# Row maxima of 80 attention branches scaled by ScalarE instead of VectorE in a two-layer decoder trunk

## The chip, the cores and the metric

One core of one Trainium2 chip runs the whole program. The metric is device microseconds (us) from start to end of one execution, and the median of several executions is compared. The engines are called by the profile's names: PE (TensorE; PEld is its weight load), DVE (VectorE), ACT (ScalarE), POOL (GpSimd) and SP (SyncE, which issues the DMAs).

## The reference, cut to what matters

A two-layer decoder trunk runs over 1024 tokens of width 1024 in float32. Layer 0 mixes sparse attention (compressed, selected and windowed branches) with sink attention. Layer 1 mixes three dilated patterns. Each layer ends in a SwiGLU FFN. Each attention branch is a softmax over masked scores, and the change concerns the row maximum in it:

```python
s = jnp.einsum('bhgqd,bhkd->bhgqk', qr_b, kw, preferred_element_type=jnp.float32) * SCALE
s = jnp.where(wmask, s, -jnp.inf)
o_win = jnp.einsum('bhgqk,bhkd->bhgqd', jax.nn.softmax(s, axis=-1), vw.astype(jnp.float32))
...
    m = jnp.max(s, axis=-1)
    if sink is not None:
        m = jnp.maximum(m, sink)
    p = jnp.exp(s - m[..., None])
```

## The kernel before

The tokens are worked in two halves of 512. Dense jobs (projections, output projections, FFN) form one stream of matmuls. The attention branches are woven into that stream in four phases: layer 0 first half, layer 0 second half, layer 1 first half, layer 1 second half. Each phase has its own list of branches:

- kind B, 8 in each half of layer 0: sink attention;
- kinds A and W, 8 each in each half of layer 0: selected blocks and the 512 window;
- kind cmp, 8 in each half of layer 0: compressed blocks (in the first half they come last);
- kind C, 16 in the first half of layer 1;
- kinds G and N, 16 each in the second half of layer 1: strided and near keys.

That makes 112 branches with a row of maxima each: 16 of kind B, 16 of cmp, and 80 of A, W, C, G and N.

For a branch, `s_issue` (line 1639) makes PE write a unit of scores to one of two PSUM banks called pS. `maxima` (line 1659) then reduces them on DVE. For all kinds but cmp, the fused operation of line 1684 adds the mask and takes the maximum over a row, starting from `FLOOR`, in one instruction (a CUSTOM_DVE instruction and a read of its accumulator in the trace). The result is a column of the small tile `m8` (SM in the trace). When the last unit is reduced, line 1700 makes a tensor_scalar on DVE: the maximum with `FLOOR` (or with the sink), times 1/STEP, written as 128x4 float16 into the tile `br["m"]` (MR in the trace). For A and W in the second half a row's scores come in two parts, so a tensor_max (line 1697) runs first.

PE then transposes MR by a matmul with the identity into a pS bank (line 1706), ACT copies that to a tile NM (line 1709), and SP writes it as a row behind the branch's queries (line 1712). Then the branch's scores are made again, transposed and with that row, and ACT takes their exponentials.

The order of every engine's instructions is fixed when the program is built, by a planner in the kernel file. Each step is a generator that yields the letter of the engine it wants next ("v" DVE, "a" ACT, "p" PE, "vg" DVE or POOL, "s" SP). `run` (line 380) always advances the step that can start first, on clocks that `account` (line 298) keeps from the cost tables of lines 257 to 259. So a step that asks for another engine shifts the planned clocks of both engines, and with them the order of everything planned later. On the chip each engine works through its list in order, and semaphores make it wait where the plan was too early.

Of the kernel before, what the change touches and what calls it, by code (L numbers as in the profile page):

```python
# [15 lines left out]
AF = mybir.ActivationFunctionType  # L16
ALU = mybir.AluOpType
# [19 lines left out]
FLOOR = -1.25e9  # L37
STEP = 32768.0
# [223 lines left out]
class Kernel:  # L262
# [1396 lines left out]
    def maxima(self, br, h, u, fin, s):  # L1659

        nc = self.nc
        if "m" not in br:
            br["m"], br["mb"] = self.MR.take(), self.SM.take()
        m8 = br["mb"].t
        np_ = br.get("np", 1)
        if br["kind"] == "cmp":
            yield "v", self.TM.when
            sm = self.TM.take()
            nc.vector.tensor_tensor(sm.t, s.t[:, 0:256].rearrange("p (b c) -> p b c", c=64),
                                    self.mCmp[:, h * HB:(h + 1) * HB], op=ALU.add)  # L1670
            s.drop()
            yield "v"
            nc.vector.tensor_reduce(out=m8[:, 0:HB], in_=sm.t, axis=AX.X, op=ALU.max)
            sm.drop()
        else:
            mc = m8[:, 0:HB * np_].rearrange("p (b c) -> p b c", c=np_)
            tab = br["maskS"] if hasattr(br["maskS"], "shape") else br["maskS"]()
            x = 0
            for il, a, w, c, left in u:
                acc = mc[:, il, c:c + 1]  # L1680
                yield "v"
                if tab.shape[1] >= left:
                    o = tab.shape[1] - left
                    nc.vector.tensor_tensor_reduce(out=self.junk[:, 0:w], in0=s.t[:, x:x + w], in1=tab[:, o:o + w],
                                                   scale=1.0, scalar=FLOOR, op0=ALU.add, op1=ALU.max, accum_out=acc)
                else:
                    nc.vector.tensor_reduce(out=acc, in_=s.t[:, x:x + w], axis=AX.X, op=ALU.max)
                x += w
            s.drop()
            br["parts"] -= 1  # L1690
            if br["parts"]:
                return
        yield "v"
        top = m8[:, 0:HB]
        if np_ > 1:

            nc.vector.tensor_max(mc[:, :, 0], mc[:, :, 0], mc[:, :, 1])
            top = mc[:, :, 0]
            yield "v"
        nc.vector.tensor_scalar(br["m"].t, top, br["sink"][1] if "sink" in br else FLOOR, 1.0 / STEP, op0=ALU.max,  # L1700
                                op1=ALU.mult)
        br["mb"].drop()
        row = self.low(br)[64 + br["row"]:65 + br["row"]]
        yield "p", self.pS.when
        ps = self.pS.take()
        nc.tensor.matmul(ps.t[0:HB, 0:P], br["m"].t, self.ident16, start=True, stop=True)
        yield "a", self.NM.when
        nm = self.NM.take()
        nc.scalar.copy(nm.t, ps.t[0:HB, 0:P])
        ps.drop()  # L1710
        yield "s"
        self.dma(row.rearrange("r (b p) -> r b p", b=HB), nm.t)
        nm.drop()
        br["ready"] = self.scope + self.o.rowlat
# [1105 lines left out]
```

## Time and profile before

| | us |
|---|---|
| median of 3 runs | 2656.15 |
| range of the runs | 2652.08 to 2656.83 |
| the profiled execution, its own time | 2659.92 |
| span of the profiled execution, first to last instruction | 2658.1 |
| mean granted TensorE clock, of full speed | 0.975 |

All work of the kernel carries one line of the code (L245) in the profile, since a helper issues it, so the groups below are told apart by engine, operation and tile: MR is the tile of scaled maxima, SM small tiles, pS, pT, pO and pD PSUM banks, S working tiles in SBUF, and PH the two halves of the probabilities. A "wait" is idle time of an engine, put down to the work that ended last before it went on.

### The profile page before, as it was taken

The page shows a single profiled execution, that of the slowest core. Times are in us where ns is not written, and L with a number is a line of the kernel's source. Part 1 is how long each engine was busy: PE and PEld are TensorE (multiplying, and loading weights), DVE is VectorE, ACT ScalarE, POOL GpSimd, SP SyncE. Part 2 cuts the span into 40 slices and gives each one's busy share as a digit, 9 for nine tenths or more (in the row PEclk, how much of TensorE's full clock was granted, in tenths as well). Part 3 has the DMA queues.
Part 4 walks back from the last instruction along what each step waited for, and adds up shares of the span by engine and source line. Part 5 has one row for each costly group of instructions (what it writes and reads, how often), then busy time and mean ns, then how long its engine had stood idle before and what let it go on. Part 6 is the DMA issues. An engine that isn't in the chain of part 4 may idle for free.

```text
span 2658.1 us, 42701 instructions
## 1 busy us (share of the span) xinstructions
PE 2514.3 (95%) x15510; PEld 1586.3 (60%) x15510; DVE 1959.7 (74%) x4445; ACT 1437.0 (54%) x2398; POOL 720.1 (27%) x511
## 2 busy tenths in 40 slices
PE   7887889899999999999999999998999999999998
PEld 7665667655555577765444477766555557754445
DVE  6798988877887788686666667888787885555554
ACT  6555656666666566544444456555566665433332
POOL 3344555301011344441000144334011114500002
PEclk8898999999999999999999999998999999999999
DMA  6465355222233234643334346685255443533320
GB/s 172 137 170 133 115 162 154 70 84 79 84 89 89 82 115 155 207 130 102 111 97 118 105 139 184 165 222 162 81 149 144 132 141 104 174 119 100 103 80 32
DMA packets 456214, 331.63 MB, mean 125 GB/s; under 512 B 54310, under 2 KB 431344, under 8 KB 456004
## 3 DMA queue, kind: packets, MB, share of 16 engines
q1 hardware_dynamic: 456004, 328.91, 42.8%
q8 instruction: 122, 2.00, 0.3%
q14 instruction: 88, 0.72, 0.1%
HBM read 273.41 MB, written 51.09 MB: 122 GB/s over the span
## 4 chain that ended last, share of the span: by engine, by line
PE 42%; DVE 9%; issue 3%; ACT 2%; DMA 2%; POOL 1%; SPq 1%; DVEq 0%; POOLq 0%; ACTq 0%
PE pD L245 38%; DVE S L245 6%; PE pS L245 2%; ACT S L245 1%; PE pT L245 1%; PE pO L245 1%; DVE SM L245 1%; POOL S L245 1%; DVE pT L245 1%; DVE junk L245 1%; SPq L245 1%; DMA S<-in_w_out_o 1%; DMA S<-xd 0%; DVE PH L245 0%; DMA S<-in_w_out_e 0%
## 5 line engine op out<-in xcount | busy, mean ns | idle before, releaser
L245 PE MATMUL pD<-S,S 128*128 128x512 f16 (+3 forms) x9648 | 2196.5, 379 | 28.6 <-DVE S L245 23.7
L245 PEld LDWEIGHTS <-S 128*128 128x128 f16 (+2 forms) x6960 | 644.6, 100 | 712.4 <-issue 87.1
L245 PEld LDWEIGHTS pD<-S,S 128*128 128x128 f32 x4272 | 732.5, 193 | 160.9 <-DVE S L245 17.4
L245 POOL TENSOR_TENSOR S<-S,S 128x512 f32<-128x512 f32 (+3 forms) x261 | 480.2, 1853 | 819.8 <-ACT S L245 682.4
L245 DVE SCALAR_TENSOR_TENSOR S<-S,wsc,S 128x1024 f16<-128x1024 f32 x224 | 295.2, 1318 | 59.3 <-ACT S L245 57.2
L245 ACT ACTIVATE S<-S 128x1024 f16<-128x1024 f32 (+4 forms) x294 | 238.1, 811 | 133.4 <-DVE S L245 131.8
L245 ACT CAST S<-S 128x512 fp32r<-128x512 f32 (+2 forms) x251 | 241.1, 1016 | 102.1 <-DVE S L245 59.0
L245 ACT ACTIVATE S<-S,wsc 128x1024 f16<-128x1024 f32 x224 | 253.5, 1141 | 50.0 <-DVE wsc L245 45.5
L245 DVE SCALAR_TENSOR_TENSOR S<-pD,SM,S 128x512 f32<-128x512 f32 x208 | 156.1, 751 | 130.1 <-PE pD L245 119.7
L245 DVE TENSOR_TENSOR S<-S,S 128x512 fp32r<-128x512 f32 (+3 forms) x149 | 191.8, 1299 | 62.0 <-ACT S L245 58.0
L245 POOL TENSOR_TENSOR PH<-S,PH 128x512 f16<-128x512 f32 (+3 forms) x76 | 94.8, 1249 | 455.5 <-ACT PH L245 323.2
L245 DVE TENSOR_TENSOR S<-pD,S 128x512 f32<-128x512 f32 (+1 forms) x238 | 157.3, 665 | 69.5 <-PE pD L245 62.3
L245 DVE TENSOR_TENSOR PH<-S,PH 128x512 f16<-128x512 f32 (+3 forms) x228 | 168.0, 741 | 43.1 <-ACT PH L245 42.0
L245 ACT ACTIVATE S<-pD,SM 128x512 f32<-128x512 f32 (+2 forms) x136 | 80.4, 604 | 198.0 <-PE pD L245 168.5
L245 ACT CAST PH<-S 128x512 f16<-128x512 f32 (+3 forms) x304 | 175.9, 586 | 9.4 <-PE pO L245 2.6
L245 PE MATMUL pT<-S,S 128*128 128x128 f16 (+11 forms) x1072 | 167.3, 279 | 11.6 <-ACT S L245 8.3
L245 ACT ACTIVATE S<-pT,jointC 128x512 f32<-128x512 f32 (+1 forms) x112 | 73.2, 655 | 165.4 <-DVE pT L245 163.8
L245 PEld LDWEIGHTS <-PH 128*128 128x128 f16 (+1 forms) x3384 | 128.3, 100 | 54.1 <-issue 16.4
L245 ACT ACTIVATE S<-pT,jointA 128x512 f32<-128x512 f32 (+1 forms) x144 | 92.1, 648 | 116.0 <-DVE pT L245 87.6
L245 PE MATMUL pO<-S,PH 128*128 128x65 f16 (+1 forms) x3192 | 133.7, 197 | 12.3 <-DVE PH L245 5.6
L245 POOL TENSOR_TENSOR S<-OS,SM 128x256 f32<-128x256 f32 x57 | 50.4, 884 | 341.2 <-DVE SM L245 291.4
L245 PE MATMUL pS<-S,S 128*128 128x256 f16 (+4 forms) x460 | 98.8, 302 | 20.4 <-DVE SM L245 14.9
(216 smaller groups left out, 1997.7 us busy)
## 6 DMA issues: line engine op xcount, KB each, us to landing
S<-in_w_gate_up SPq DMA_DIRECT2D x176, 512.0 KB
S<-in_w_down SPq DMA_DIRECT2D x88, 512.0 KB
S<-in_w_qkv_o SPq DMA_DIRECT2D x48, 512.0 KB
S<-in_w_in_e SPq DMA_DIRECT2D x22, 512.0 KB
xd<-S SPq DMA_DIRECT2D x32, 256.0 KB
S<-in_w_out_e SPq DMA_DIRECT2D x16, 512.0 KB
S<-xd SPq DMA_DIRECT2D x32, 256.0 KB
S<-in_w_out_o SPq DMA_DIRECT2D x16, 512.0 KB
```

Of the source, the lines that this page charges most:

```text
L245: return fn(*a, **kw)
```

## The change

The scaling of line 1700 is given to ACT for the branches that have neither a sink nor kind cmp (A, W, C, G and N). It becomes an activation Copy with scale 1/STEP. The maximum with `FLOOR` is left out there, since the fused operation starts from it. The yields before it ask for ACT instead of DVE. The tensor_max of two parts stays on DVE.

```diff
-        yield "v"
+        yield "v" if np_ > 1 or "sink" in br or br["kind"] == "cmp" else "a"
         top = m8[:, 0:HB]
         if np_ > 1:
 
             nc.vector.tensor_max(mc[:, :, 0], mc[:, :, 0], mc[:, :, 1])
             top = mc[:, :, 0]
-            yield "v"
-        nc.vector.tensor_scalar(br["m"].t, top, br["sink"][1] if "sink" in br else FLOOR, 1.0 / STEP, op0=ALU.max,
-                                op1=ALU.mult)
+            yield "v" if "sink" in br else "a"
+        if "sink" in br or br["kind"] == "cmp":
+            nc.vector.tensor_scalar(br["m"].t, top, br["sink"][1] if "sink" in br else FLOOR, 1.0 / STEP, op0=ALU.max,
+                                    op1=ALU.mult)
+        else:
+            nc.scalar.activation(br["m"].t, top, AF.Copy, scale=1.0 / STEP)
         br["mb"].drop()
```

## Rows read from the trace of the kernel before

**Rows 1.** The page's first two parts: busy time of each engine with its share of the span and its instructions, and the granted TensorE clock in 40 slices of the span.

```profile
PE 2514.3 (95%) x15510; PEld 1586.3 (60%) x15510; DVE 1959.7 (74%) x4445; ACT 1437.0 (54%) x2398; POOL 720.1 (27%) x511
...
PEclk8898999999999999999999999998999999999999
```

**Rows 2.** Busy time of the engines by stage: stretch, its length, then busy us and instructions of PE, PEld, DVE, ACT and POOL, the granted clock, the DMA share and GB/s. 181 to 346 is kinds A and W of the first half of layer 0, 475 to 1000 the second half (A, W, cmp), 1000 to 1143 projections, 1143 to 1745 kind C and 1745 to 2184 kinds G and N.

```profile
181.00:346.00 165.00, 136.57 (x1065) 98.42 (x1063) 146.57 (x347) 102.18 (x187) 87.15 (x61) 0.93 0.48 126
...
475.00:1000.00 525.00, 512.33 (x3626) 296.27 (x3625) 417.68 (x1078) 342.54 (x572) 115.79 (x89) 1.00 0.30 88
1000.00:1143.00 143.00, 134.94 (x729) 110.56 (x728) 107.76 (x185) 80.99 (x110) 67.74 (x40) 0.99 0.56 178
1143.00:1745.00 602.00, 579.49 (x3292) 360.84 (x3291) 429.10 (x783) 283.34 (x420) 141.79 (x91) 0.99 0.46 131
1745.00:2184.00 439.00, 422.96 (x2829) 249.92 (x2826) 358.56 (x1001) 271.27 (x477) 91.90 (x77) 0.97 0.51 142
```

**Rows 3.** The same columns in stretches of 10 us inside the first of these stages.

```profile
250.00:260.00 10.00, 4.74 (x50) 3.42 (x48) 9.92 (x19) 6.63 (x11) 8.37 (x6) 0.96 0.78 185
260.00:270.00 10.00, 7.75 (x44) 5.33 (x45) 7.59 (x13) 6.39 (x14) 2.16 (x2) 0.69 0.62 179
...
310.00:320.00 10.00, 5.82 (x31) 3.57 (x29) 9.82 (x16) 6.07 (x14) 10.00 (x6) 1.00 0.20 52
320.00:330.00 10.00, 9.15 (x69) 6.64 (x70) 8.89 (x28) 4.75 (x10) 1.54 (x4) 0.83 0.42 112
```

**Rows 4.** Instructions that write or read the tile MR, by stage: PE, PEld, DVE and ACT busy, then clock, DMA share and GB/s. Up to 1143 the DVE instructions here are writes of MR alone.

```profile
181.00:346.00 165.00, 3.35 (x15) 1.20 (x15) 8.75 (x15) 0.83 (x2) 0.93 0.48 126
346.00:394.00 48.00, 1.96 (x9) 0.72 (x9) 3.49 (x9) 0.00 (x0) 0.98 0.54 167
...
475.00:1000.00 525.00, 5.22 (x24) 1.93 (x24) 8.64 (x24) 0.88 (x3) 1.00 0.30 88
```

**Rows 5.** Instructions that write or read MR in the whole span: count, then min/median/max of the duration in ns, first and last start, and form.

```profile
L245 DVE TENSOR_SCALAR MR<-SM x96: 134/167/1568, 181.1 to 2182.6; 128x4 f16<-128x4 f32 x96
...
L245 ACT ACTIVATE SM<-MR,sinks,jointB x16: 389/391/426, 129.2 to 503.0; 128x4 f32<-128x4 f16 x16
L245 ACT CAST OG<-MR x16: 198/201/207, 1745.6 to 2210.3; 128x4 f32<-128x4 f16 x16
```

**Rows 6.** Groups of instructions by form: count, busy us, mean ns of one, idle before.

```profile
L245 DVE TENSOR_SCALAR MR<-SM 128x4 f16<-128x4 f32 x96 | 33.5, 348 | 0.7
```

**Rows 7.** Waits of PE in 181 to 346: total us, times, longest.

```profile
PE pS L245 <- DVE MR L245: 8.9, 3, 3.8
PE pT L245 <- ACT S L245: 5.0, 5, 2.7
PE pS L245 <- DVE SM L245: 3.9, 6, 0.8
PE pO L245 <- DVE PH L245: 3.7, 5, 1.0
```

**Rows 8.** Waits in the whole span: PE on the tile MR, on DVE's reductions (which free the pS banks) and on ACT, and ACT on DVE.

```profile
PE pS L245 <- DVE SM L245: 36.5, 30, 6.3
PE pS L245 <- DVE MR L245: 12.4, 9, 3.8
PE pT L245 <- ACT S L245: 9.3, 10, 2.7
PE pS L245 <- ACT S L245: 8.1, 3, 5.6
...
ACT S L245 <- DVE pT L245: 276.7, 155, 7.9
```

**Rows 9.** Timeline around the first long wait of PE on MR: start, duration, engine, operation, count, and in brackets the idle time before with its releaser.

```profile
255.67 6.50 POOL L245 TENSOR_TENSOR S<-S,S 128x512 fp32r<-128x512 f32 x3
...
256.39 0.39 ACT L245 ACTIVATE S<-pD 127x256 f32<-127x256 f32 x1
...
256.94 0.07 DVE L245 DVE_READ_ACCUMULATOR2_ANT SM<- 128x1 f32 x1
256.94 4.10 DVE L245 TENSOR_TENSOR S<-S,S 128x512 fp32r<-128x512 f32 x2
...
260.96 1.23 DVE L245 TENSOR_SCALAR MR<-SM 128x4 f16<-128x4 f32 x1
262.11 0.62 DVE L245 TENSOR_TENSOR pT<-pT,tDE 128x128 f32<-128x128 f32 x2
...
262.25 0.26 PE L245 MATMUL pS<-ident,MR 128*4 128x128 f16 x1 [3.72 <-DVE MR L245]
262.43 0.69 ACT L245 ACTIVATE S<-pT,jointA 128x512 f32<-128x512 f32 x1 [5.64 <-DVE pT L245]
```

**Rows 10.** The same around the second and the third long wait.

```profile
290.18 0.08 DVE L245 DVE_READ_ACCUMULATOR2_ANT SM<- 128x1 f32 x1
290.30 0.82 DVE L245 TENSOR_SCALAR MR<-SM 128x4 f16<-128x4 f32 x1
...
291.18 0.22 PE L245 MATMUL pS<-ident,MR 128*4 128x128 f16 x1 [1.33 <-DVE MR L245]
...
318.94 1.22 DVE L245 TENSOR_SCALAR MR<-SM 128x4 f16<-128x4 f32 x1
318.98 0.37 ACT L245 COPY OS<-pO 128x260 f32<-128x260 f32 x1
...
320.21 0.22 PE L245 MATMUL pS<-ident,MR 128*4 128x128 f16 x1 [3.80 <-DVE MR L245]
```

## The prediction

> **What bounds the kernel now.** I read the page's busy times first. PE is busy 95% of the span, DVE 74%, ACT 54% [rows 1]. So a microsecond is gained only where PE idles or where its clock is below full. Next I read the stages. From 475 to 1000 PE is busy 512.33 of 525 us, and from 1143 to 2184 it lacks 39 us of 1041. In 181 to 346, however, it lacks 28.4 of 165 us, DVE is busy 146.57 (89%), POOL 87.15, and the granted clock is 0.93 [rows 2]. That is the first phase, where kinds A and W run, and it is the one stage in which the step to be moved plainly holds PE. There PE waits 8.9 us in three pieces for DVE's write of MR, the largest entry of its list [rows 7], of 12.4 us in nine pieces over the whole span [rows 8]. Last I read the timeline around those three waits [rows 9, 10], to see why DVE was late.
>
> The step is cheap when nothing disturbs it, 0.134 us at the least and 0.167 us at the median, but it has taken up to 1.568 us [rows 5]. Over 96 writes the mean is 0.348 us, in sum 33.5 us [rows 6]. In 181 to 346 fifteen of them take 8.75 us, a mean of 0.58 [rows 4]. The long ones lie where POOL works: the write at 260.96 ends at 262.19, and the POOL group that began at 255.67 ends at 262.17 [rows 9]. ACT instructions on the same small tile don't stretch: 0.198 to 0.207 us for one, 0.389 to 0.426 for the other [rows 5].
>
> **The change part by part.** Removed from DVE are 80 writes: 16 of A and W in the first half, 16 in the second, 48 in layer 1. Of the 33.5 us, 16 cmp writes stay. The fifteen of 181 to 346 all go (8.75). In 346 to 394 there are 8 cmp and one W, of which I take a ninth (0.4 of 3.49). In 475 to 1000 two thirds go (16 of 24, 5.8 of 8.64) [rows 4]. Layer 1's 48 are what remains, 33.5 - 8.75 - 3.49 - 8.64 = 12.6 us. In sum DVE loses some 27.5 us. Added to ACT are 80 activations of 128x4. The nearest row is its copy of MR itself, 0.201 us [rows 5], so 16 us.
>
> *The direct waits.* In the first, the last reduction has been read at 257.01 us. DVE then does two 128x512 subtractions, stretched to 4.10 us, before it reaches the write at 260.96, while ACT has nothing from 256.78 to 262.43 and PE waits 3.72 us [rows 9]. ACT could write MR at about 257.3, so the wait goes whole: 3.7 us. In the second the reduction ends at 290.26, and the write takes 0.82 us; 0.2 on ACT and a short hop bring PE forward by about 0.4 of the 1.33 us. In the third the write takes 1.22 us, but ACT is in the midst of other work (a copy at 318.98), so I put 0.6 of the 3.80 us [rows 10]. That is 4.7 us of the 8.9. Outside the stage 12.4 - 8.9 = 3.5 us in six pieces are left, some of kinds that stay; I take 1.0. Sum -5.7 us, with ends at 0 (the planner places another wait there) and -12.4 (all go).
>
> *DVE's shorter queue.* In 181 to 346 PE also waits in 16 pieces for DVE's reductions, DVE's PH and ACT's exponentials (3.9, 3.7 and 5.0 us) [rows 7], and these stand behind DVE's queue, directly or through ACT. If each had one moved write of 0.58 us ahead of it, 9.3 us would go; at the other end nothing, since few have one just ahead. I take a third, -3 us. Elsewhere the undisturbed write is 0.16 us and PE hardly idles, so I cost it at nothing. What hides it is the dense matmul stream; where that cover is gone (1000 to 1143, PE lacking 8 us [rows 2]) no branch of the 80 runs but the first of kind C.
>
> *The clock.* Behind the stretch in which PE is busy only 4.74 of 10 us, the next has a granted clock of 0.69, and behind 5.82 of 10 the next has 0.83 [rows 3]. Each is a mix of the two levels, 1.2 and 2.4 GHz. The first loses at most 3.1 us, the second 1.7. Part of the idle time before each would go, though not all; I take a third of 4.8, -1.5 us, ends 0 and -4.8.
>
> *What ACT takes back.* 16 us more lie on an engine that is idle 63 us in 181 to 346 and 168 us in 1745 to 2184 [rows 2]. The hop from DVE to ACT is short: DVE's first addition of the pair at 262.11 ends near 262.42, and ACT starts at 262.43 [rows 9]. The new wait is that of ACT for the reductions. ACT takes its list in order, so behind a scaling that waits stand exponentials, copies that free pO and pS, and weight splits, and PE waits for those. PE's waits on ACT's S tiles are 9.3 + 8.1 us in 13 pieces, beside 276.7 us in which ACT waited for DVE's pT [rows 8]: 6% of such waiting reaches PE. The ends are 0 and +16 (each of the 80 on PE's path). I take +1, near the lower end, because of that 6% of 16. SP is not passed: the DMA of the row follows the same copy as before. What is replanned beside it, POOL's share of the "vg" steps included, has no sign that the trace shows. I bound it by the two largest PE waits named outside the reductions' rows, 5.6 and 3.8 us [rows 8], coming or going: 9 us either way.
>
> Among these rows one rule speaks against the change. The Trainium skill (Perfetto Trace Analysis, Optimizing Scalar/DVE Operations) says that where the vector engine has a performance mode for an operation it is the faster place for it, and that moving pays when it is saturated. The undisturbed durations agree, 0.167 against 0.201 us; by them alone 80 moves would cost 2.7 us of engine time. The mean of 0.348 us [rows 6] disagrees, and by it the move frees 11.5 us in all. The same skill (SBUF — State Buffer, Who interferes with whom) states that a vector instruction in a two-port mode and a GpSimd one exclude each other for a whole instruction; that would make the stretched writes an effect of POOL's work, which the row at 260.96 bears out.
>
> *Sum:* -5.7 - 3 - 1.5 + 1 = -9.2 us. The profiled execution took 2659.92 us, 1.8 more than its span and 3.8 more than the median. From 2659.92 the sum gives 2650.7; from the median, 2656.15 - 9.2 = 2647.
>
> **The rivals.**
> 1. *The gain is given back; no change.* The planner books the write at only 72 ns on DVE and knows no stretching by POOL, so with DVE's clock freed it may hand DVE other steps, and DVE stays as late in 181 to 346 as it is. The waits change their name from MR to SM and PH. For it: PE's waits on DVE's reductions are already 36.5 us, three times those on MR [rows 8]. Against it: the wait at 258.5 has an idle ACT beside it [rows 9]. It gives about 2655, from 2651 to 2661.
> 2. *ACT's order becomes the bound; slower.* ACT reaches a scaling whose reduction is late, and the exponential behind it is late too, so PE waits for the probabilities. Its place is 181 to 346, where DVE runs behind, and 1745 to 2184, where most of the branches are. For it: ACT already waits 1.8 us at a time for DVE's pT, 155 times [rows 8]. Against it: only 6% of that reached PE. The price is up to 0.2 us for each of the 80, +16 us. It outweighs the gains of 10.2 us when about 50 of the 80 reach PE whole, and with the replanned order adding up to 9 us, with fewer. The case runs from 2662 to 2672; I put 2665.
> 3. *The change doesn't do what it says.* If few branches met the condition, the time would stay at 2656. The kinds are plain from the code, 80 of 112, so I give it next to nothing, inside the first rival.
>
> **How the numbers follow.** The forecast gets 0.52, the first rival 0.25, the second 0.23. The forecast's own range is 2630 to 2650: its far end adds up the better ends (12.4 + 9.3 + 4.8 = 26.5 us). For 8 times in 10 I go from 2632 to 2667, which leaves a tenth on either side: below it, all gains with a lucky order; above it, the upper part of the second rival. A difference of 0.2% (5.3 us) is about what a measurement of this kernel can tell from none. So faster 0.52, same 0.25, slower 0.23.
>
> **What would show it.** Right: ACT has 80 activations that write MR, near 0.2 us each and unstretched, 16 writes of MR from SM are left on DVE, DVE's busy time falls by about 27 us and ACT's grows by about 16. In the first A and W phase, PE's waits on MR fall from 8.9 us to about 4, its idle time falls from 28 us, and the granted clock rises above 0.93. The stages after 475 keep their length within 2 us. Wrong: PE waits as long there, for DVE's reductions or PH (first rival), or for ACT's S and MR (second). The prediction is also wrong if a stage without any of the 80 changes its length by more than 3 us, for then the replanned order has decided, and not the moved step.

## The result, and the profile after

| | before | after |
|---|---|---|
| median | 2656.8 us | 2636.7 us (5 runs, 2632.9 to 2642.1) |
| ratio | | 0.993, 95% interval 0.9909 to 0.9951 |
| the profiled execution, its own time | 2659.92 us | 2636.47 us |
| span | 2658.1 us | 2634.8 us |
| mean granted clock | 0.975 | 0.979 |

(The median of before is that of the runs beside those of after.) The changed kernel is 0.7% faster, some 18 to 20 us. 9.2 us were forecast: the sign is right and the time lies in the range, but the gain is twice as large, so part of it comes from somewhere that the sum did not look. (The two profiled executions differ by more, some 23 us, since that of before lies 3.1 us above its median.)

First the page of the changed kernel, its busy times and the granted clock by slice, which answer to [rows 1]:

```profile
PE 2499.8 (95%) x15510; PEld 1579.3 (60%) x15510; DVE 1944.9 (74%) x4370; ACT 1448.4 (55%) x2478; POOL 718.9 (27%) x506
...
PEclk8999989999999999999999999999999999999999
```

ACT has 80 instructions more, and 11.4 us more of busy time. DVE has 75 fewer (POOL has five fewer too, so five steps came to DVE from there) and only 14.8 us less. The clock's slices below 9 are the first and the sixth; before they were 1, 2, 4 and 28, and the last of these, at 1800 us, is gone.

The instructions that write MR, with min/median/max in ns, and the groups with their sum and mean, of the changed kernel (before: [rows 5, 6]):

```profile
L245 ACT ACTIVATE MR<-SM x80: 188/205/227, 179.7 to 2160.2; 128x4 f16<-128x4 f32 x80
L245 DVE TENSOR_SCALAR MR<-SM x16: 141/160/1303, 341.4 to 978.9; 128x4 f16<-128x4 f32 x16
```

```profile
L245 DVE TENSOR_SCALAR MR<-SM 128x4 f16<-128x4 f32 x16 | 4.6, 287 | 0.1
...
L245 ACT ACTIVATE MR<-SM 128x4 f16<-128x4 f32 x80 | 16.2, 203 | 32.0 <-DVE SM L245 31.3
```

None of the 80 is stretched on ACT: the longest takes 0.227 us. The 16 that stayed on DVE still reach 1.303. So the moved step costs 16.2 us on ACT, where it had cost some 33.5 - 4.6 = 28.9 us on DVE. (The Trainium skill, SBUF — State Buffer, Who interferes with whom, states that ACT waits for no other engine's access; the 188 to 227 ns agree.)

The waits of PE in the first phase of the changed kernel (before: [rows 7]) and the stretch itself (before: [rows 2]):

```profile
PE pS L245 <- DVE SM L245: 5.7, 4, 3.4
PE pT L245 <- ACT S L245: 3.6, 5, 1.0
PE pT L245 <- DMA S<-NM: 3.4, 3, 1.6
...
PE pO L245 <- DVE PH L245: 0.4, 1, 0.4
```

```profile
181.00:346.00 165.00, 143.91 (x1130) 105.58 (x1129) 145.38 (x341) 106.55 (x205) 92.52 (x67) 0.95 0.50 130
```

No wait on MR is left there (8.9 us before). PE is busy 143.9 instead of 136.6 of the 165 us, and the clock is 0.95 instead of 0.93. Over the whole span, PE's waits on the reductions and on MR are these (before: [rows 8]):

```profile
PE pS L245 <- DVE SM L245: 31.0, 18, 6.3
...
PE pS L245 <- ACT MR L245: 3.5, 2, 1.9
...
PE pS L245 <- DVE MR L245: 2.0, 2, 1.5
```

So far this is the forecast. To see where the other half was won, I counted the instructions of PE on pD, the dense stream, in order of their start, and asked when each kernel had started the same one. (Every trace here holds the same 15510 matmuls, 9688 of them on pD, so the counts are exact.)

| dense matmuls started | before | after | after - before |
|---|---|---|---|
| 420 (no branch of the 80 yet) | 174.1 us | 172.1 us | -2.0 |
| 1150 | 477.2 | 464.8 | -12.4 |
| 2950 | 999.3 | 984.6 | -14.7 |
| 3550 | 1131.8 | 1118.1 | -13.7 |
| 5950 | 1711.0 | 1701.8 | -9.2 |
| 6500 | 1893.3 | 1870.2 | -23.1 |
| 7700 | 2218.8 | 2195.3 | -23.5 |
| 9600 | 2634.1 | 2610.7 | -23.4 |

Two places win: the stage with A and W of the first half (10.4 us) and the one in which the last phase, with G and N, begins (13.9 us). What lies between them, 1150 to 5950, loses 3.2 us. Two executions of the kernel before differ by 3.9 us between the 3550th and the 5950th alone, so that loss is not shown to be the change's.

These are the stretches of 10 us at the beginning of the last phase, of pD alone, in the kernel before (PE, PEld, DVE and ACT busy, clock, DMA share, GB/s):

```profile
1790.00:1800.00 10.00, 7.43 (x31) 5.49 (x31) 0.27 (x1) 0.00 (x0) 1.00 1.03 278
1800.00:1810.00 10.00, 0.92 (x4) 0.39 (x3) 0.69 (x1) 0.00 (x0) 0.78 0.80 197
1810.00:1820.00 10.00, 0.00 (x0) 0.00 (x0) 0.00 (x0) 0.00 (x0) 0.50 0.51 135
1820.00:1830.00 10.00, 7.25 (x22) 4.78 (x23) 0.69 (x1) 0.00 (x0) 0.70 0.46 126
```

and in the changed kernel:

```profile
1780.00:1790.00 10.00, 7.75 (x34) 5.69 (x32) 0.69 (x1) 0.00 (x0) 1.00 0.51 160
1790.00:1800.00 10.00, 9.71 (x39) 7.17 (x40) 0.69 (x1) 0.00 (x0) 1.00 0.00 0
1800.00:1810.00 10.00, 7.79 (x34) 5.53 (x30) 0.69 (x1) 0.00 (x0) 1.00 0.26 67
1810.00:1820.00 10.00, 5.67 (x20) 0.00 (x0) 0.68 (x1) 0.00 (x0) 0.86 0.42 127
```

Before, the dense stream stands still for 20 us; PE has only attention work, and the clock falls to 0.50 of full speed, the lower (1.2 GHz) of its two levels. After, no stretch is without dense work. PE's list has 161 attention matmuls in that place, and the piece that the stream needs next, the last one of the norm's input to the FFN, comes late from DVE (timeline of before, DVE and then PE; the second of the three dense matmuls waits for that piece, which ends at 1821.60):

```profile
1791.06 0.75 DVE L245 SCALAR_TENSOR_TENSOR S<-S,gains,S 128x512 fp32r<-128x512 f32 x1
...
1820.85 0.75 DVE L245 SCALAR_TENSOR_TENSOR S<-S,gains,S 128x512 fp32r<-128x512 f32 x1
...
1821.04 1.83 PE L245 MATMUL pD<-S,S 128*128 128x512 f32 x3
```

ACT's half of that piece was done at 1803.7. DVE was hardly idle in between: its list has attention steps there. The old plan puts 30 us between the last two pieces, the new plan 12 (1774 and 1786 us). This is an order written when the program is built, so the experiments have to keep the order and the engine apart.

### The profile page after: what moved, and what is told of

Read it like the earlier page. It is cut to its first block, busy times and chain, and to the rows that moved or that the text cites. A ratio compares the mean times of both kernels' runs of the same rounds, so it can differ in the third digit from the quotient of the medians.

```text
span 2634.8 us, 42704 instructions
## 1 busy us (share of the span) xinstructions
PE 2499.8 (95%) x15510; PEld 1579.3 (60%) x15510; DVE 1944.9 (74%) x4370; ACT 1448.4 (55%) x2478; POOL 718.9 (27%) x506
## 4 chain that ended last, share of the span: by engine, by line
PE 46%; DVE 8%; issue 3%; ACT 2%; DMA 1%; POOL 1%; SPq 0%; DVEq 0%; POOLq 0%; ACTq 0%
PE pD L245 41%; DVE S L245 6%; PE pS L245 2%; ACT S L245 2%; PE pT L245 1%; PE pO L245 1%; POOL S L245 1%; DVE SM L245 1%; DVE pT L245 0%; DVE junk L245 0%; DMA S<-in_w_out_o 0%; DMA S<-xd 0%; DMA S<-in_w_out_e 0%; DMA chk<-S 0%; DMA chq<-S 0%
## 5 line engine op out<-in xcount | busy, mean ns | idle before, releaser
L245 DVE TENSOR_TENSOR S<-S,S 128x512 fp32r<-128x512 f32 (+4 forms) x151 | 194.3, 1302 | 70.1 <-ACT S L245 65.7
L245 POOL TENSOR_TENSOR PH<-S,PH 128x512 f16<-128x512 f32 (+2 forms) x73 | 95.6, 1313 | 423.6 <-ACT PH L245 295.6
L245 PE MATMUL pT<-S,S 128*128 128x128 f16 (+11 forms) x1072 | 165.2, 276 | 14.7 <-ACT S L245 8.1
L245 PEld LDWEIGHTS <-PH 128*128 128x128 f16 (+1 forms) x3384 | 127.3, 99 | 56.0 <-issue 19.6
L245 DVE SCALAR_TENSOR_TENSOR S<-S,gains,S 128x512 fp32r<-128x512 f32 (+1 forms) x80 | 98.7, 1249 | 23.3 <-ACT S L245 22.3
```

The lines of the kernel that those rows point to most:

```text
L245: return fn(*a, **kw)
```

## The experiments

Theory 1: the step's place on DVE cost the time (it is stretched there, or stands in the queue), so ACT as the engine brings the gain. Theory 2: the planner's new order brings it. The runs of before that stood beside these had medians of 2657.1 or 2657.2 us.

**The old order, executed on ACT.** The planner books the step on DVE as before; only the instruction goes to ACT.

```diff
+            self.account("v", "tensor_scalar", (br["m"].t, top), {})
+            nc.scalar.real.activation(br["m"].t, top, AF.Copy, scale=1.0 / STEP)
```

> The 80 scalings run on ACT, but the planner books them as DVE steps, so PE's, SP's and POOL's lists are those of before, and the scaling stands in ACT's list where the old plan issued it. Theory of execution (DVE's stretched writes and its queue are what the change saves): 2647 us, 9 below before, PE's waits on MR in 181 to 346 down from 8.9 to about 4. Theory of the order (the new plan, above all that around 1800 us, brings the gain): 2656 within 4, and the 20 us with PE on no dense matmul at 1801 to 1821 stay.

Measured: 2649.7 us, ratio 0.9968 (0.9956 to 0.9981). The time lies between the two theories, nearer the first; the pause stays, 19.6 us from 1782.5 us on.

**The new order, executed on DVE.** The reverse: booked on ACT, executed on DVE.

```diff
+        yield "v" if np_ > 1 or "sink" in br or br["kind"] == "cmp" else "a"
...
+            self.account("a", "activation", (br["m"].t, top), {})
+            nc.vector.real.tensor_scalar(br["m"].t, top, FLOOR, 1.0 / STEP, op0=ALU.max, op1=ALU.mult)
```

> The scalings run on DVE, but the planner books them as ACT steps, so the lists are those of the changed kernel but for the place of the scaling itself. Theory of execution: the gain is mostly lost, 2648 us or more, since the writes are stretched again. Theory of the order: 2637 to 2643, the stretch of 1700 to 1850 as short as in the changed kernel.

Measured: 2652.9 us, ratio 0.9979 (0.9966 to 0.9992). Neither half is the whole: with the old order 7 us are won by the engine alone, with the old engine 4 us by the order alone, and both together win 18 to 20. The MR group of this run shows that the step is stretched as before, and its wait is back:

```profile
L1705 DVE TENSOR_SCALAR MR<-SM x80: 153/164/1561, 183.1 to 2177.1; 128x4 f16<-128x4 f32 x80
```

```profile
PE pS L245 <- DVE MR L1705: 16.4, 16, 2.4
```

**Only the first phase** (kinds A and W, first half of layer 0), and **only the last phase** (kinds G and N), each booked and executed on ACT. This is the first; the second has `moved = br["kind"] in "GN"`:

```diff
+        moved = br["kind"] in "AW" and h == 0
+        yield "v" if np_ > 1 or not moved else "a"
```

> Only the 16 scalings of A and W in the first half of layer 0 go to ACT, the other 64 stay on DVE; everything behind them is planned anew. Theory of execution: 2647 us, since the stretched writes that held PE all lie there. Theory of the order: the stage of 181 to 346 gains up to 10 us, and what follows may come out anywhere within 10 us of before.

> Only the 32 scalings of G and N (second half of layer 1) go to ACT, so all up to about 1720 us is as before. Theory of execution: 2655 us, since PE waited only some 1 us for MR there. Theory of the order: 2640 to 2646, the dense stream no longer stops at 1800 us.

Measured: 2649.0 us, ratio 0.9972 (0.9962 to 0.9983), and 2645.8 us, ratio 0.9956 (0.994 to 0.9971). So the 16 steps of the first phase bring some 8 us and the 32 of the last some 11, together the whole. The forecast had all but 1.0 us of its gain in the first.

**The kernel before, once more**, as a control.

> The kernel before itself once more, for a second profile and the spread of one and the same program. All theories: ratio 1 within 0.15%. Theory that the slow clock of 1800 to 1830 belongs to the old order: the clock is below 0.8 there again. Theory that it is an accident of one execution: it is not.

Measured: 2656.8 us, ratio 1.0003 (0.9993 to 1.0013). The slow clock of the last phase is there again (all engines, same columns as in rows 2):

```profile
1800.00:1810.00 10.00, 5.96 (x69) 5.13 (x68) 9.05 (x28) 7.53 (x16) 4.01 (x3) 0.72 0.54 145
1810.00:1820.00 10.00, 7.95 (x78) 5.68 (x78) 9.37 (x38) 4.47 (x11) 3.72 (x5) 0.67 0.50 143
```

So the pause belongs to the program, and not to one execution of it.

**The old order on DVE, but by a form of instruction that is not stretched.** The fused operation multiplies by 1/STEP itself, and a reduction over one element takes the place of the scaling step in 72 of the 80.

```diff
-                                                   scale=1.0, scalar=FLOOR, op0=ALU.add, op1=ALU.max, accum_out=acc)
+                                                   scale=r, scalar=FLOOR * r, op0=ALU.add, op1=ALU.max, accum_out=acc)
...
+            self.account("v", "tensor_scalar", (br["m"].t, top), {})
+            nc.vector.real.tensor_reduce(out=br["m"].t, in_=top[:, :, None], axis=AX.X, op=ALU.max)
```

> Old order, and the step stays on DVE, but 72 of the 80 (not A in the second half of layer 0) become a tensor_reduce over one element, with the scale put into the fused operation before it. Theory that the stretching by POOL is what hurts, and that the reduction form escapes it: no write above 0.25 us, and 5 to 8 us faster than before. Theory that DVE's queue is what hurts (the place in the list, not the duration): within 3 us of before, since DVE still has the 80 steps.

Measured: 2647.7 us, ratio 0.9968 (0.9956 to 0.9981), the ratio that ACT gave with the same order. Its tile MR:

```profile
L1707 DVE TENSOR_REDUCE MR<-SM x72: 120/149/178, 178.8 to 2176.8; 128x4 f16<-128x4 f32 x72
L245 DVE TENSOR_SCALAR MR<-SM x24: 149/169/1292, 341.1 to 988.1; 128x4 f16<-128x4 f32 x24
```

The reduction stands at the same places of DVE's list, behind the same work, and never takes more than 0.178 us, though 17 of the 72 overlap an instruction of POOL; the scalings that are left in the same run reach 1.292. So no other engine is needed for a gain: it was won by a form that POOL does not stretch. (The Trainium skill, SBUF — State Buffer, Who interferes with whom, states that on trn2 this reduction has no two-port mode and so never contends with GpSimd; the 178 ns agree.)

That POOL does the stretching, the trace of before shows for the scalings: each of the 23 writes of MR in [rows 5] that take over 0.3 us ends 22 to 28 ns after an instruction of POOL that it overlapped, and 71 of the 73 shorter ones overlap none.

But the place in DVE's list costs too. In 181 to 346, PE's waits on MR fall from 8.9 to 5.5 us with the reduction, and to 3.0 with ACT in the same order (this run, then the old order on ACT):

```profile
PE pS L245 <- DVE MR L1707: 5.5, 3, 3.0
```

```profile
PE pS L245 <- ACT MR L1705: 3.0, 3, 2.1
```

The first of these waits is the one of [rows 9]. The reduction takes 0.14 us there, but behind the same two subtractions, so that 3.01 of the 3.72 us stay:

```profile
254.22 4.11 DVE L245 TENSOR_TENSOR S<-S,S 128x512 fp32r<-128x512 f32 x2
258.25 0.14 DVE L1707 TENSOR_REDUCE MR<-SM 128x4 f16<-128x4 f32 x1
258.45 0.27 PE L245 MATMUL pS<-ident,MR 128*4 128x128 f16 x1 [3.01 <-DVE MR L1707]
```

The profiled execution of this run is the slowest of its nine (2654.1 us), that of the old order on ACT the fastest of its twelve (2639.8), so these two traces can't show where the gain of the medians lies.

**Another order of the kernel before.** The latency that the planner gives a DVE instruction is 228 or 232 ns instead of 230. The work and the engines stay.

> The kernel before with one number of the planner changed, the latency it books after a DVE step, 228 ns instead of 230: same work, on the same engines, in a new order. Theory that a new order by itself is worth nothing on average: within 10 us of before, either way. Theory that the old order was a poor draw and nearly any other is better: 5 us or more faster.

> The same with 232 ns. Theory of the draw: the same side as at 228. Theory of no average effect: within 10 us of before, either way, not bound to the side of the run at 228.

Measured: 2657.7 us, ratio 1.0001 (0.9992 to 1.0011), and 2662.1 us, ratio 1.0021 (1.0012 to 1.003). A new order is not a gain by itself; both of these keep the pause.

**The last phase's new order, executed on DVE.**

> The planner books the scaling steps of the last phase (kinds G and N) on ScalarE, so that it makes the order of the run that moved only this phase, but VectorE executes them. If the gain of that run (2645.8 us, some 11 us, nearly all at 1733 to 1840 us) is the order's, which puts the step that lets the dense work go on ahead of the attention steps, this run takes 2643 to 2649 us and the stretch 1800 to 1830 us shows a granted clock of 0.9 or more. If it is the engine's, it takes 2653 to 2659 us. Half of each gives about 2651 us.

Measured: 2653.1 us, ratio 0.9979 (0.9969 to 0.9989): about a third of the gain. The time lies at the edge of the range that was set for the engine, while the clock, 1.00 in all stretches from 1780 to 1840, is the sign set for the order, so neither theory alone is right. The pause is gone. What is lost comes later. Here are the stretches between the 6500th and the 7700th dense matmul, of the run with the step on ACT and of this one (all engines):

```profile
1876.30:2201.20 324.90, 322.74 (x2273) 176.70 (x2272) 261.02 (x765) 212.24 (x391) 55.91 (x51) 1.00 0.48 134
```

```profile
1886.00:2216.10 330.10, 323.28 (x2272) 176.55 (x2271) 263.75 (x785) 210.52 (x370) 55.97 (x51) 1.00 0.49 133
```

With ACT PE lacks 2.2 us of this stretch, with DVE 6.8. Between the two runs, PE's list is the same, and 4.9 us of the difference arise in five places, each time at a transpose of MR: PE waits there 1.12, 0.41, 1.28, 0.63 and 1.06 us for DVE (the trace names MR twice and wsc, DVE's next step, three times), where with ACT it does not wait. The third of them, with the step on DVE and then on ACT:

```profile
1973.53 1.93 DVE L245 SCALAR_TENSOR_TENSOR S<-S,wsc,S 128x1024 f16<-128x1024 f32 x1
1975.37 0.16 DVE L1706 TENSOR_SCALAR MR<-SM 128x4 f16<-128x4 f32 x1
1975.59 0.22 PE L245 MATMUL pS<-ident,MR 128*4 128x128 f16 x1 [1.28 <-DVE MR L1706]
```

```profile
1962.19 1.92 DVE L245 SCALAR_TENSOR_TENSOR S<-S,wsc,S 128x1024 f16<-128x1024 f32 x1
1962.31 0.20 ACT L245 ACTIVATE MR<-SM 128x4 f16<-128x4 f32 x1 [0.51 <-DVE SM L245]
1962.90 0.22 PE L245 MATMUL pS<-ident,MR 128*4 128x128 f16 x1
```

So here it is DVE's list that costs: the scaling itself is not stretched (0.16 us), but stands behind another step. The run with the whole new order on DVE loses at the same five places, within 0.02 us each, against the changed kernel. The counts of all runs show the same by stages (one trace each):

| length in us of the stage between dense matmuls | 420 to 1150 | 5950 to 6500 | 6500 to 7700 |
|---|---|---|---|
| before; repeated; latency 228; 232 | 303.1, 300.7, 304.1, 301.7 | 182.4, 179.9, 181.9, 179.2 | 325.5, 325.4, 326.2, 326.2 |
| old order, on ACT | 292.3 | 176.0 | 325.6 |
| only the first phase on ACT | 294.2 | 180.2 | 325.5 |
| old order, reduction on DVE | 299.0 | 178.9 | 324.7 |
| new order, on DVE | 300.4 | 170.3 | 330.7 |
| new order of the last phase, on DVE | 303.2 | 168.1 | 330.2 |
| the same, on ACT | 300.7 | 166.6 | 324.9 |
| the changed kernel; with latency 228 | 292.7, 298.4 | 168.4, 170.8 | 325.1, 325.0 |

In the first stage the runs that have the step on ACT there take 292 to 294 us and those with the scaling on DVE 300 to 303, whatever the order (at 228 ns it is 298 and 304). The beginning of the last phase takes 167 to 171 us in the new order, on either engine, and 176 to 182 in the old. In the rest of the phase the new order costs 5 us more with the step on DVE than on ACT. That is why the halves don't add up.

**The changed kernel in another order** (latency 228):

> The changed kernel, planned with 228 instead of 230 ns for a VectorE operation: the same work on the same engines in another order. If the order of the changed kernel is a lucky one, this loses the part of the gain that booking gave (about 5 to 11 us) and takes 2642 to 2650 us. If moving the steps makes good orders in general, it takes 2633 to 2641 us.

Measured: 2643.6 us, ratio 0.995 (0.9937 to 0.9962). It keeps some two thirds of the gain, in the range that was set for a lucky order; its interval overlaps that of the changed kernel.

**No scaling step in 72 of the 80.** There the fused operation scales and accumulates straight into MR as f16; the other 8 (A of the second half) are scaled by ACT. With 230 ns the planner finds no order, so this run has 228, and a second one has 230 with 246 instead of 250 ns for ACT.

```diff
-                acc = mc[:, il, c:c + 1]
+                acc = br["m"].t[:, il:il + 1] if one and np_ == 1 else mc[:, il, c:c + 1]
...
-                                                   scale=1.0, scalar=FLOOR, op0=ALU.add, op1=ALU.max, accum_out=acc)
+                                                   scale=r, scalar=FLOOR * r, op0=ALU.add, op1=ALU.max, accum_out=acc)
```

> In 72 of the 80 branches no scaling step is left on any engine: the fused operation on VectorE multiplies by 1/STEP itself and accumulates its maximum straight into the tile of maxima in f16 (the branches with two pieces take one maximum of the two into it). The planner gets 228 ns for a VectorE operation, since with 230 it finds no order. If what counts is that the short, stretched VectorE operation is gone and its place in the list is free, this should do at least what moving it did without a new order (2648 to 2650 us) and, if the new order is as good as that of the changed kernel, 2630 to 2640 us. If the new order is a poor one, up to 2655 us.

Measured: 2688.6 us, ratio 1.0117 (1.0104 to 1.0131). This was a miss: with 72 steps fewer it is the slowest kernel of all. Its stretches of pD alone:

```profile
1840.00:1850.00 10.00, 0.91 (x4) 0.39 (x3) 0.68 (x1) 0.00 (x0) 0.72 0.23 62
1850.00:1860.00 10.00, 0.00 (x0) 0.00 (x0) 0.00 (x0) 0.00 (x0) 0.67 0.67 177
1860.00:1870.00 10.00, 0.00 (x0) 0.00 (x0) 0.69 (x1) 0.00 (x0) 0.50 0.36 94
1870.00:1880.00 10.00, 0.00 (x0) 0.00 (x0) 0.00 (x0) 0.00 (x0) 0.67 0.56 141
1880.00:1890.00 10.00, 4.94 (x13) 0.00 (x0) 0.00 (x0) 0.00 (x0) 0.56 0.51 129
```

The dense stream pauses for some 40 us. That pause can be read without a chip. In PE's own list of instructions, weight loads included, I counted the longest runs of attention work without one instruction on pD. All the runs above with the old order in the last phase have the 314 there, and those with the new one none over 96 in that phase.

| kernel | longest runs without dense work | where, by dense matmuls before it | median |
|---|---|---|---|
| before | 314 | 6221 | 2657 us |
| changed | 98, 96 | 920, 6104 | 2637 us |
| scale folded, latency 228 | 300, 208, 479 | 488, 6221, 6296 | 2689 us |
| scale folded, ACT latency 246 | 98, 169 | 488, 6314 | below |

> The kernel with the scale folded into the fused operation again, with the same work on the same engines, but planned with 230 ns for a VectorE and 246 ns for a ScalarE operation, so that its lists come out in another order. In TensorE's own list the longest runs of attention work without one dense matmul are the sign to read: the kernel before has one of 314 instructions in the last phase, the changed kernel none over 96, the first folded kernel 300 in the first phase and 208 and 479 in the last (it lost 30 us there), this one 98 and 169. If the order made the first folded kernel slow, this one takes 2636 to 2650 us: the stretched step gone, some 8 us, and all or most of the 17 us of the long pause. If folding itself costs (the f16 accumulator, or a maximum that is read later), it stays above 2670 us.

Measured: 2645.9 us, ratio 0.9958 (0.9944 to 0.9972), as expected if the order is the cause: the same work in another order is 43 us faster. It does not beat the changed kernel: against it, its trace is 9.8 us longer between the 420th and 1150th dense matmuls, 8.4 up to the 2950th and 4.3 between the 5950th and 6500th, and 8.3 shorter between the 2950th and 3550th. Its own pause, of pD alone:

```profile
1820.00:1830.00 10.00, 0.97 (x3) 0.00 (x0) 0.00 (x0) 0.00 (x0) 0.75 0.57 144
1830.00:1840.00 10.00, 4.34 (x18) 0.00 (x0) 0.69 (x1) 0.68 (x1) 0.74 0.45 118
```

## Why the prediction was right, and where it was short

**The mechanism held, with two parts to it.** The step came late on DVE because POOL stretched it, and because it stood behind other work of DVE, as the prediction's reading of the first wait has it. The signs named for it in the first phase came: 80 activations near 0.2 us, 16 writes left, no long wait on MR in the first phase, the clock there at 0.95. The reduction on DVE gained by its median as much as ACT did in the same order (both ratios 0.9968, 0.9956 to 0.9981), so the stretching has a price of its own; the waits of 5.5 us that stayed in its trace are the list's. How the first phase's gain divides between the two is not shown.

**The first phase** was sized about right. The direct waits, DVE's queue and the clock made -10.2 us, all but 1.0 of it there. The stage from 420 to 1150 dense matmuls is 10.4 us shorter than before and 8.0 shorter than in its repetition, and the run that moves this phase alone gained 8 us by its median. The direct term was too cautious: no wait on MR is left where 4 us were expected to stay. The queue's term was right in sum: PE's waits on the reductions, on DVE's PH and on ACT's exponentials were 12.6 us and are 9.7, and -3 was forecast. But the one on the reductions grew, from 3.9 to 5.7 us, and others grew or came in, that on the row's DMA from 1.8 to 3.4. Neither rival came about. Of the 8.9 us that the first wanted renamed, a part may be such growth; for the second, PE's wait on ACT's MR is 3.5 us in two pieces, far from 16.

**The step that failed** is "Elsewhere the undisturbed write is 0.16 us and PE hardly idles, so I cost it at nothing", together with the replanned order, which was said to have "no sign that the trace shows". The last phase brought 11 us. The trace of before did show the place: 20 us without a dense matmul at a clock of 0.50 to 0.78. I had read the stage from 1745 to 2184 as one row, in which 16 us of idle time and 0.97 of the clock look harmless [rows 2], and the page's 8 in slice 28 [rows 1] was not followed up. The term of 9 us for the order was taken from two waits, while the pause itself, about 20 us of PE without its main work, holds the 14 us by which this stage became shorter. That the range held was luck in this part: its far end had added up better ends of other terms, most of them of the first phase. "The stages after 475 keep their length within 2 us" was wrong. The prediction's own test of the order, a stage with none of the 80 that changes by over 3 us, missed it: from 2950 to 3550 dense matmuls the projections took 133.5 us instead of 132.5, since the order decided in a stage that has some of the 80.

**DVE's busy time** was to fall by 27 us and fell by 14.8, though the 80 steps took some 28.9 us of it with them. Other instructions took longer instead: in the groups by form of the changed kernel, the 1024-wide subtraction has a mean of 1546 ns, where it had 1434, and the FFN norm's piece 1181, where it had 1116; and five steps came over from POOL.

```profile
L245 DVE TENSOR_TENSOR S<-S,S 128x1024 fp32r<-128x1024 f32 x38 | 58.5, 1546 | 6.2 <-ACT S L245 6.1
L245 DVE SCALAR_TENSOR_TENSOR S<-S,gains,S 128x512 fp32r<-128x512 f32 x48 | 56.6, 1181 | 23.3 <-ACT S L245 22.3 <-POOL S L245 0.8
```

**What stays open.** Which part of the first phase's gain is the stretching's and which the list's. With ACT in the old order the beginning of the last phase took 176.0 us, though the pause of 20 us is still in it, and some 3 us less than any other run of that order; why is not shown. How much of the gain is a lucky order's: at 228 ns the changed kernel takes 7 us more, and its trace is 5.7 us longer in the first stage and 2.4 at the beginning of the last phase. Why this change led the planner to the better order, rather than to a worse one, was not tried: in the kernel before, 2 ns more or less did not lead it there.

## What to carry to other kernels

Before costing a change at nothing in a stage, cut the stage into stretches of 10 us and look at the main stream alone: a pause of 20 us, with the clock down to half, disappears in a row of 440 us. Where a planner writes the order, any change of a step's engine is two changes; book it one way and execute it the other to see each, and read the longest runs without main work from the program's own lists, which can tell a poor order before anything has run. And a tiny vector operation beside a busy GpSimd is priced by its mean and its maximum, not its median: another form of instruction on the same engine takes the stretching away, while only another engine takes the step out of that engine's list.

## What the runs showed of the hardware

In the kernel before, a 128x4 scaling on DVE took 0.134 to 1.568 us, and each one over 0.3 us ended 22 to 28 ns after an instruction of POOL that it overlapped. A 128x4 reduction at the same place of the list took 0.120 to 0.178, with POOL at work or not, and an activation 0.187 to 0.264 over the runs. The accumulator of the fused operation could be written as f16 into the final tile at hardly any cost: its read took 0.085 us instead of 0.082. The executions of one kernel lie up to 19 us apart (2639.8 to 2658.9 us in 12 runs of the old order on ACT), so each difference of times above rests on the ratios, and on medians of 4 to 12 runs; the stage lengths rest on one trace each.
